# Two low parts of the up weights from VectorE to GpSimd, and the last epilogue's rows in another ring and queue: one core of Trainium2, a diffusion layer step

## The chip, the cores and the metric

The kernel runs on one core of one Trainium2 chip. The metric is the device time in microseconds (us) of one execution. Durations come from one profiled execution; the runs without a profile give the median.

## The reference

One layer of a flow-matching backbone in inference: a normalised input projection, eight heads of neighbourhood attention beside eight heads of an RWKV-7 scan, an output projection with a gated residual, and then the stage that this change touches, a gated feed-forward network with a width-3 convolution between, a residual and a last norm:

```python
D_MODEL = 1024
SEQ = 256
DEC_SEQ = 2048
D_FF = 2816
...
def _rmsnorm(x, g):
    xf = x.astype(jnp.float32)
    y = xf * lax.rsqrt(jnp.mean(xf * xf, axis=-1, keepdims=True) + EPS)
    return (y * g.astype(jnp.float32)).astype(x.dtype)
...
def _conv_ffn(h, w1, w3, wc, w2):
    return (jax.nn.silu(_dwconv(h @ w1, wc)) * (h @ w3)) @ w2
...
    h2 = _rmsnorm(x, norm2) * (1 + sc2) + sh2
    x = x + g2 * _conv_ffn(h2, *fp)
...
    y_prompt = _rmsnorm(xp, norm_f)
    y_sample = _rmsnorm(xs, norm_f)
```

`_dwconv` is the convolution of width 3 along the tokens; context (256) and latent tokens (2048) go through the same weights. All inputs and outputs are fp32. The kernel keeps fp32 accuracy on TensorE by splitting each operand of a product into a high part in the shorter format fp32r and a low part, the rest: three matmuls, high x high, low x high and high x low, stand for one.

## The kernel before, in words

Stages run one after the other; the feed-forward stage, `ffn`, takes the last 1760 us. It goes over three blocks of 768 tokens (`b`), and in each over 22 groups of 128 hidden features (`f`).

For one f, `up` (L447) makes both projections at once with seven products of quarter matrices in place of eight (a Strassen scheme), each of 4 x 3 matmuls: 84 matmuls at L456, out of sums of quarters of the weights (`PRODUCTS` names them: 11, S2, S1, 12, S3, S4, 22). VectorE puts the results together at L465 to L474, GpSimd one at L475. Of these L465 frees the PSUM tile into which a later product goes. Then `gate` (L477): the convolution `conv3` (ACT at L114, VectorE at L116), Silu on ACT (L481), the gate product on VectorE (L483, L484), and the split of the result into `gh` (ACT, L36) and `gl` (VectorE, L46). `down` (L492) multiplies it with the rows of w2: six token tiles of 6 matmuls (L499), whose PSUM tiles VectorE adds to `yacc` (L507; at a block's first f it copies them, L505). The down of f is issued behind the up of f + 1.

`UpWeights.fetch` (L334) loads the weights of the next f on the sync queue, into a ring of three tiles `wr`: r1 (columns of w1, L339), r3 (columns of w3, L340), r2 (rows of w2, L342). r1 is the quarters 11 and 12, r3 is 21 and 22. GpSimd makes the sums S1 to S4 (L354, L355, L357, L361), partly in place. `put` splits each of the seven weights: ACT writes the high part `wh` (L36), and the engine that `put` is given subtracts it to get the low part `wl` (L46). GpSimd also makes the low part `w2l` of the w2 rows. `wh` and `wl` have eight tiles each.

`tokens` (L386) prepares the next block's activations (`hT`, `lT`, `h`, `l`) when a block begins, out of `part` tiles: a ring `st` of six tiles of 128 x 512, which `up` uses as well.

`epilogue` (L421) ends a block: for each of six token tiles and two halves it loads the rows of x with `short` (L427) on the GpSimd queue into one of two tiles `e` (and, for the first two token tiles, the gate's rows), multiplies yacc by the gate (L437), adds x (L438), squares and sums on ACT (L439, which writes into the x tile, so that tile is free only then), and scales by the norm (L440 to L443). L444 stores it on the sync queue. For blocks 0 and 1 these steps are generated between the down tiles of f = 1 of the next block; for block 2 they come behind everything.

The order of instructions on each engine is not the written one: a list scheduler of the tile framework decides it, so that an edit of one engine's work can move that of others. Each engine runs its own row in order, and waits where an operand or a free tile isn't there.

Of the kernel before, what the change touches and what calls it, by code (L numbers as in the profile page):

```python
# [7 lines left out]
F32 = mybir.dt.float32  # L8
# [34 lines left out]
def split(hi_eng, lo_eng, hi, lo, src):  # L43

    copy(hi_eng, hi, src)
    lo_eng.tensor_sub(lo, src, hi)  # L46
# [15 lines left out]
class Weights:  # L62
# [21 lines left out]
    def fetch(self):  # L84

        self.load()
        if not self.raw:
            return
        r = self.raw.pop(0)
        hi = self.pool.tile([128, KT, 128], F32R, name="wh", bufs=self.ahead + 1)  # L90
        lo = self.pool.tile([128, KT, 128], F32R, name="wl", bufs=self.ahead + 1)
        split(self.nc.scalar, self.lo_eng, hi, lo, r)
        self.ready.append((hi, lo))
# [52 lines left out]
def xrows(xp, xs, t):  # L146

    return xp[t * 128 : t * 128 + 128, :] if t < 2 else xs[(t - 2) * 128 : (t - 1) * 128, :]
# [177 lines left out]
class UpWeights:  # L326
# [7 lines left out]
    def fetch(self, f):  # L334

        nc, pool, KH = self.nc, self.pool, KT // 2
        cols = slice(f * 128, f * 128 + 128)
        r1, r3, r2 = (pool.tile([128, KT, 128], F32, name="wr", bufs=3) for _ in range(3))
        nc.sync.dma_start(r1, self.wv[0][:, :, cols])  # L339
        nc.sync.dma_start(r3, self.wv[1][:, :, cols])  # L340
        r2 = r2.rearrange("p c f -> p (c f)")
        nc.sync.dma_start(r2, self.w2[cols, :])  # L342
        a11, a12, a21, a22 = r1[:, :KH], r1[:, KH:], r3[:, :KH], r3[:, KH:]
        out = {}

        def put(n, src, eng):
            h = pool.tile([128, KH, 128], F32R, name="wh", bufs=AHEAD)
            l = pool.tile([128, KH, 128], F32R, name="wl", bufs=AHEAD)
            split(nc.scalar, eng, h, l, src)
            out[n] = (h, l)  # L350

        s3 = pool.tile([128, KH, 128], F32, name="s3", bufs=1)
        put("11", a11, nc.vector)
        nc.gpsimd.tensor_sub(s3, a11, a21)  # L354
        nc.gpsimd.tensor_add(a21, a21, a22)  # L355
        put("S1", a21, nc.gpsimd)
        nc.gpsimd.tensor_sub(a21, a21, a11)  # L357
        put("S2", a21, nc.gpsimd)
        put("12", a12, nc.vector)
        put("S3", s3, nc.gpsimd)  # L360
        nc.gpsimd.tensor_sub(a12, a12, a21)  # L361
        put("S4", a12, nc.gpsimd)
        put("22", a22, nc.gpsimd)
        w2h = pool.tile([128, D], F32R, name="w2h")
        w2l = pool.tile([128, D], F32R, name="w2l")
        split(nc.scalar, nc.gpsimd, w2h, w2l, r2)
        self.ready.append((out, (w2h, w2l)))


def ffn(tc, W, rows_d, eps, wc, norm_f, h2, x1_d, yp, ys):  # L370
    nc = tc.nc
    hv = h2.rearrange("(k c p) n -> k p c n", k=2, p=128)
    KH = KT // 2
    with tc.tile_pool(name="c1", bufs=1) as c1, tc.tile_pool(name="c2", bufs=2) as c2, tc.tile_pool(
        name="cp", bufs=1, space=PSUM
# [6 lines left out]
        def part(n):  # L382

            return c2.tile([128, 512], F32, name="st", bufs=6)[:, :n]
# [36 lines left out]
        def epilogue(b, yacc):  # L421

            halves = [slice(q * 512, q * 512 + 512) for q in range(2)]

            def short(src):
                t = c2.tile([128, 512], F32, name="e")
                nc.gpsimd.dma_start(t, src)  # L427
                return t

            for t in range(6):  # L430
                tok = b * 6 + t
                y = yacc[t]
                r = c2.tile([128, 4], F32, name="rf")
                for q, s in enumerate(halves):
                    g = g2[:, s] if tok >= 2 else short(rows_d[3, 0:1, s].to_broadcast([128, 512]))
                    x = short(x1_d[tok * 128 : tok * 128 + 128, s])
                    nc.vector.tensor_mul(y[:, s], y[:, s], g)  # L437
                    nc.vector.tensor_add(y[:, s], y[:, s], x)  # L438
                    nc.scalar.activation(x, y[:, s], AF.Square, accum_out=r[:, q : q + 1])  # L439
                nc.vector.tensor_add(r[:, 2:3], r[:, 0:1], r[:, 1:2])  # L440
                nc.scalar.activation(r[:, 3:4], r[:, 2:3], AF.Sqrt, bias=eps, scale=1.0 / D)
                nc.vector.reciprocal(r[:, 2:3], r[:, 3:4])
                nc.vector.scalar_tensor_tensor(y, y, r[:, 2:3], nf, op0=ALU.mult, op1=ALU.mult)  # L443
                nc.sync.dma_start(xrows(yp, ys, tok), y)  # L444
                yield
# [1128 lines left out]
```

## Time and profile before

| what | us |
|---|---|
| median of three runs | 4527.84 (4527.21 to 4528.01) |
| profiled execution | 4528.56 |
| its span on the core | 4526.8 |
| TensorE busy in the span | 3852.0 |
| feed-forward stage | about 2767 to 4527 |
| one f in block 0, in blocks 1 and 2 | 25.42, 23.35 |

Engines: PE is TensorE's matmul, PEld its weight load, DVE is VectorE, POOL is GpSimd, SP (SPq) the sync engine's queue. A line such as L456 is that of the kernel before. The time of one f is the distance of two equal instructions of neighbouring f's. Busy shares are averages over stages with different limits, so the stretches are shown apart below.

### The profile page before, as it was taken

How to read it: one execution, taken by the hardware profiler on the slowest of the kernel's cores; microseconds unless marked ns; L12 is line 12 of the kernel's file. 1: busy time of each engine (PE TensorE's matmuls, PEld its weight loads, DVE VectorE, ACT ScalarE, POOL GpSimd, SP SyncE). 2: the span in 40 equal slices, each digit the busy share in tenths (PEclk: the TensorE clock that was granted, in tenths of full speed). 3: DMA queues.
4: the chain of work that ended last, by engine and by line, in shares of the span. 5: the costliest groups of instructions: out<-in, count | busy, mean ns of one | idle time of the engine just before them, and what ended most of it. 6: DMA issues, size and time to landing. Idle time of an engine off the chain costs nothing. (4 is left out here: it accounts for less than half of the span.)

```text
span 4526.8 us, 78134 instructions
## 1 busy us (share of the span) xinstructions
PE 3852.0 (85%) x29954; PEld 3414.9 (75%) x29954; DVE 3115.0 (69%) x4658; ACT 1845.9 (41%) x3728; POOL 2323.6 (51%) x1879
## 2 busy tenths in 40 slices
PE   6798987888388887899886886999988999889996
PEld 6787877777266666788775665888877999779995
DVE  4325586868577774566664224888888888878887
ACT  2421254544377773455442223333334333343332
POOL 0334344545234336555664444666656776667662
PEclk9899998989599997999998997999988999999998
DMA  5787545453756623323343443221223222232222
GB/s 211 243 280 212 145 117 165 114 159 112 178 116 135 128 58 102 86 76 81 95 102 105 167 149 94 61 66 61 66 80 112 68 64 70 84 106 63 70 70 66
DMA packets 682387, 513.24 MB, mean 113 GB/s; under 512 B 234691, under 2 KB 612612, under 8 KB 677916
## 3 DMA queue, kind: packets, MB, share of 16 engines
q1 hardware_dynamic: 508444, 378.64, 30.0%
q10 hardware_dynamic: 170080, 118.06, 8.8%
q0 software_dynamic: 3488, 11.54, 0.8%
q8 instruction: 236, 3.87, 0.4%
q14 instruction: 139, 1.14, 0.1%
HBM read 369.85 MB, written 139.76 MB: 113 GB/s over the span
## 5 line engine op out<-in xcount | busy, mean ns | idle before, releaser
L46 POOL TENSOR_TENSOR wl<-wr,wh 128x512 fp32r<-128x512 f32 (+1 forms) x349 | 613.2, 1758 | 575.3 <-ACT wh L36 503.8
L55 PE MATMUL g<-h,wh 128*128 128x384 f32 (+1 forms) x2592 | 641.8, 359 | 32.3 <-DVE r L116 8.4
L36 ACT ACTIVATE wh<-wr 128x512 fp32r<-128x512 f32 (+1 forms) x485 | 336.3, 704 | 500.2 <-DMA wr<-in_w_ffn_dram 210.1
L55 PEld LDWEIGHTS g<-h,wh 128*128 128x128 f32 x2592 | 487.6, 200 | 67.1 <-issue 27.7
L507 DVE TENSOR_TENSOR yacc<-yacc,yp 128x512 f32<-128x512 f32 x756 | 479.3, 680 | 28.9 <-PE yp L499 5.2
L456 PE MATMUL u<-hT,wh 128*128 128x386 f32 x1056 | 366.8, 347 | 38.3 <-DVE st L465 24.8
L456 PE MATMUL u<-lT,wh 128*128 128x386 f32 x1056 | 364.4, 345 | 12.2 <-DVE lT L46 12.2
L456 PE MATMUL u<-hT,wl 128*128 128x386 f32 x1056 | 364.4, 345 | 3.8 <-POOL wl L46 3.8
L55 PE MATMUL g<-h,wl 128*128 128x384 f32 (+1 forms) x1296 | 359.9, 355 | 0.0
L499 PE MATMUL yp<-w2h,gh 128*128 128x512 f32 x792 | 273.1, 418 | 48.6 <-DVE yacc L507 20.0
L46 DVE TENSOR_TENSOR wl<-wr,wh 128x512 fp32r<-128x512 f32 (+1 forms) x136 | 251.9, 1853 | 63.2 <-ACT wh L36 63.1
L456 PE MATMUL u<-h,wh 128*128 128x386 f32 x792 | 272.7, 344 | 19.3 <-ACT h L36 17.5
L456 PE MATMUL u<-l,wh 128*128 128x386 f32 x792 | 271.7, 345 | 8.2 <-DVE l L46 7.9
L456 PE MATMUL u<-h,wl 128*128 128x386 f32 x792 | 274.4, 346 | 0.0
L499 PE MATMUL yp<-w2l,gh 128*128 128x512 f32 x792 | 257.8, 404 | 0.0
L499 PE MATMUL yp<-w2h,gl 128*128 128x512 f32 x792 | 257.0, 403 | 0.0
L55 PEld LDWEIGHTS g<-h,wl 128*128 128x128 f32 x1296 | 250.8, 200 | 2.8 <-issue 2.5
L456 PEld LDWEIGHTS u<-hT,wh 128*128 128x128 f32 x1056 | 203.0, 192 | 51.8 <-DVE st L465 31.9
L499 PEld LDWEIGHTS yp<-w2h,gh 128*128 128x128 f32 x792 | 151.6, 193 | 108.9 <-DVE yacc L507 50.1
L354 POOL TENSOR_TENSOR s<-wr 128x512 f32<-128x512 f32 x66 | 85.8, 1300 | 271.3 <-DMA wr<-in_w_ffn_dram 271.3
L456 PEld LDWEIGHTS u<-lT,wh 128*128 128x128 f32 x1056 | 203.4, 193 | 17.8 <-DVE lT L46 17.5
L1273 DVE TENSOR_TENSOR X<-iv,mmask 128x256 f16<-128x256 f32 x360 | 146.3, 422 | 98.7 <-PE iv L1270 93.8
(333 smaller groups left out, 10085.3 us busy)
## 6 DMA issues: line engine op xcount, KB each, us to landing
wr<-in_w_ffn_dram SPq DMA_DIRECT2D x198, 512.0 KB
wr<-in_w_in_dram ACTq DMA_DIRECT2D x45, 512.0 KB
wr<-in_w_in_dram ACTq DMA_DIRECT2D x72, 256.0 KB
d_ar<-ar SPq DMA_DIRECT2D x24, 768.0 KB
d_bk<-bk SPq DMA_DIRECT2D x24, 768.0 KB
kd<-d_ks SPq DMA_DIRECT2D x32, 576.0 KB
bk<-d_bk SPq DMA_DIRECT2D x72, 256.0 KB
ar<-d_ar SPq DMA_DIRECT2D x288, 64.0 KB
```

What stands on the lines that cost most here:

```text
L36: eng.activation(dst, src, AF.Copy, scale=1.0 if scale is None else scale)
L46: lo_eng.tensor_sub(lo, src, hi)
L55: nc.tensor.matmul(ps[q][:, : e - a], A[:, c, :], B[c][:, a:e], start=c == 0 and n == 0, stop=c == KT - 1 and n == 2)
L354: nc.gpsimd.tensor_sub(s3, a11, a21)
L456: nc.tensor.matmul(acc[q], A[a][x][:, c, :], T[t][c][y], start=i < 3 and c == 0 and n == 0, stop=c == KH - 1 and n == 2, skip_group_check= ...
L499: nc.tensor.matmul(yps[q], A[:, t * 128 : t * 128 + 128], B[:, q * 512 : q * 512 + 512], start=n == 0, stop=n == 2)
L507: nc.vector.tensor_add(d, d, yps[q])
L1273: nc.vector.tensor_mul(half(X1, n), X, mk)
```

## The change

In `fetch` the low parts of the weights "11" and "12" are made by GpSimd, as those of the five others are. In `epilogue` the rows of x of the last block (b = 2) are loaded by the sync queue into the ring of six `st` tiles; in blocks 0 and 1 they stay in two `e` tiles on the GpSimd queue. The lines from L426 on are one higher in the changed kernel.

```diff
--- before.py
+++ after.py
@@ -350,13 +350,13 @@
             out[n] = (h, l)
 
         s3 = pool.tile([128, KH, 128], F32, name="s3", bufs=1)
-        put("11", a11, nc.vector)
+        put("11", a11, nc.gpsimd)
         nc.gpsimd.tensor_sub(s3, a11, a21)
         nc.gpsimd.tensor_add(a21, a21, a22)
         put("S1", a21, nc.gpsimd)
         nc.gpsimd.tensor_sub(a21, a21, a11)
         put("S2", a21, nc.gpsimd)
-        put("12", a12, nc.vector)
+        put("12", a12, nc.gpsimd)
         put("S3", s3, nc.gpsimd)
         nc.gpsimd.tensor_sub(a12, a12, a21)
         put("S4", a12, nc.gpsimd)
@@ -423,8 +423,9 @@
             halves = [slice(q * 512, q * 512 + 512) for q in range(2)]
 
             def short(src):
-                t = c2.tile([128, 512], F32, name="e")
-                nc.gpsimd.dma_start(t, src)
+
+                t = part(512) if b == 2 else c2.tile([128, 512], F32, name="e")
+                (nc.sync if b == 2 else nc.gpsimd).dma_start(t, src)
                 return t
 
             for t in range(6):
```

On VectorE, one f in the middle of block 0, around the gate product. `u_34468` is the PSUM tile that L465 empties, `t_34408` the gate's tile of this f, `t_34626` that of the next. Before:

```order
L507 TENSOR_TENSOR yacc_31746<-yacc_31746,yp_34398 128x512
L507 TENSOR_TENSOR yacc_31746<-yacc_31746,yp_34399 128x512
L46 TENSOR_TENSOR wl<-wr,wh 128x512
L483 TENSOR_TENSOR t_34408<-st,t_34408 128x386
L484 TENSOR_TENSOR t_34408<-st,t_34408 128x382
L46 TENSOR_TENSOR gl<-t_34408,gh 128x768
L465 TENSOR_TENSOR st<-st,u_34468 128x386
L46 TENSOR_TENSOR wl<-wr,wh 128x512
L116 SCALAR_TENSOR_TENSOR t_34626<-u_34467,wct,t_34626 128x255
L470 TENSOR_TENSOR st<-st,u_34468 128x386
```

and in the changed kernel (L484, L485, L466 and L471 are L483, L484, L465 and L470 of before):

```order
L508 TENSOR_TENSOR yacc_31746<-yacc_31746,yp_34398 128x512
L508 TENSOR_TENSOR yacc_31746<-yacc_31746,yp_34399 128x512
L484 TENSOR_TENSOR t_34408<-st,t_34408 128x386
L485 TENSOR_TENSOR t_34408<-st,t_34408 128x382
L46 TENSOR_TENSOR gl<-t_34408,gh 128x768
L466 TENSOR_TENSOR st<-st,u_34468 128x386
L116 SCALAR_TENSOR_TENSOR t_34626<-u_34467,wct,t_34626 128x255
L471 TENSOR_TENSOR st<-st,u_34468 128x386
```

Both `wl` are gone from the row, so that the first L483 stands right behind the additions to yacc; the rest keeps its order.

On GpSimd, the round of one f near the end of block 0 (`s_36610` is the tile of S3, L475 the addition that `up` gives to GpSimd). Before:

```order
L354 TENSOR_TENSOR s_36610<-wr 128x512
L355 TENSOR_TENSOR wr<-wr 128x512
L46 TENSOR_TENSOR w2l<-wr,w2h 128x1024
L46 TENSOR_TENSOR wl<-wr,wh 128x512
L357 TENSOR_TENSOR wr<-wr 128x512
L46 TENSOR_TENSOR wl<-wr,wh 128x512
L361 TENSOR_TENSOR wr<-wr 128x512
L46 TENSOR_TENSOR wl<-s_36610,wh 128x512
L46 TENSOR_TENSOR wl<-wr,wh 128x512
L475 TENSOR_TENSOR st<-st 128x386
L46 TENSOR_TENSOR wl<-wr,wh 128x512
```

and in the changed kernel:

```order
L354 TENSOR_TENSOR s_36610<-wr 128x512
L355 TENSOR_TENSOR wr<-wr 128x512
L46 TENSOR_TENSOR w2l<-wr,w2h 128x1024
L46 TENSOR_TENSOR wl<-wr,wh 128x512
L357 TENSOR_TENSOR wr<-wr 128x512
L46 TENSOR_TENSOR wl<-wr,wh 128x512 x2
L361 TENSOR_TENSOR wr<-wr 128x512
L46 TENSOR_TENSOR wl<-s_36610,wh 128x512
L46 TENSOR_TENSOR wl<-wr,wh 128x512
L476 TENSOR_TENSOR st<-st 128x386
L46 TENSOR_TENSOR wl<-wr,wh 128x512 x2
```

The low part of "12" stands beside that of S2 (x2), ahead of L361, and that of the next f's "11" beside that of "22" at the end, where the round waits for the load that L354 reads.

On GpSimd, in the transition from block 0 to block 1, where the epilogue of block 0 loads its rows (L427). Before:

```order
L354 TENSOR_TENSOR s_37310<-wr 128x512
L355 TENSOR_TENSOR wr<-wr 128x512
L46 TENSOR_TENSOR w2l<-wr,w2h 128x1024
L427 DMA e<-d_rows 128x512
L427 DMA e<-d_x_64 128x512
L427 DMA e<-d_rows 128x512
L475 TENSOR_TENSOR st<-st 128x386
L427 DMA e<-d_x_64 128x512 x8
L46 TENSOR_TENSOR wl<-wr,wh 128x512
L357 TENSOR_TENSOR wr<-wr 128x512
L46 TENSOR_TENSOR wl<-wr,wh 128x512
L427 DMA e<-d_x_64 128x512
```

and in the changed kernel (L428 is L427 of before):

```order
L354 TENSOR_TENSOR s_37310<-wr 128x512
L355 TENSOR_TENSOR wr<-wr 128x512
L46 TENSOR_TENSOR wl<-wr,wh 128x512
L357 TENSOR_TENSOR wr<-wr 128x512
L46 TENSOR_TENSOR w2l<-wr,w2h 128x1024
L46 TENSOR_TENSOR wl<-wr,wh 128x512
L428 DMA e<-d_rows 128x512
L46 TENSOR_TENSOR wl<-wr,wh 128x512
L361 TENSOR_TENSOR wr<-wr 128x512
L428 DMA e<-d_x_64 128x512
L46 TENSOR_TENSOR wl<-s_37310,wh 128x512
L428 DMA e<-d_rows 128x512
```

Before, eight loads of x stand in a row ahead of the weights of f = 2; now the low parts and sums of that f are mixed with the loads. On the sync queue the end changes too: behind the last weights come ten loads of x, the first store of yacc, two loads and the other five stores, where before there were six stores.

## Rows read from the trace of the kernel before

**Rows 1.** The page's first table: busy time, share of the span and instructions of each engine.

```profile
PE 3852.0 (85%) x29954; PEld 3414.9 (75%) x29954; DVE 3115.0 (69%) x4658; ACT 1845.9 (41%) x3728; POOL 2323.6 (51%) x1879
```

**Rows 2.** The busy time of each engine in six stretches of the span: block 0 from f = 2 on, the change from block 0 to 1, block 1, the change from block 1 to 2, block 2, and the end behind the last matmul. Columns: stretch, its us, then busy us (and instructions) of PE, PEld, DVE, ACT and POOL, the mean granted clock of TensorE, the DMA engines' busy share and GB/s.

```profile
2830.00:3337.00 507.00, 480.85 (x2398) 429.79 (x2397) 418.51 (x540) 171.47 (x282) 315.76 (x221) 1.00 0.21 64
3337.00:3461.00 124.00, 90.43 (x362) 75.35 (x362) 105.34 (x151) 52.37 (x101) 67.01 (x59) 0.79 0.37 119
3461.00:3905.00 444.00, 443.94 (x2280) 409.86 (x2279) 376.14 (x475) 160.85 (x268) 312.63 (x210) 1.00 0.23 69
3905.00:4069.00 164.00, 127.14 (x568) 110.71 (x567) 133.76 (x188) 69.17 (x130) 98.53 (x77) 0.89 0.30 96
4069.00:4428.00 359.00, 359.00 (x1837) 330.40 (x1836) 306.29 (x389) 126.14 (x212) 249.29 (x169) 1.00 0.23 70
4493.00:4527.00 34.00, 0.00 (x0) 0.00 (x0) 22.03 (x40) 10.99 (x29) 4.83 (x9) 0.54 0.51 170
```

**Rows 3.** The chain of waits that ended last: two rows of block 0, then two of block 1. Columns: start in us, us, what.

```profile
3237.28 2.72 DVE wl L46
3262.70 2.72 DVE wl L46
3718.51 14.90 PE u L456 x84
3733.41 8.45 PE yp L499 x36
```

**Rows 4.** What TensorE waited for in 2970 to 3330 us (block 0, 14 f's). Columns: engine, tile and line that waited, what it waited for: us in total, times, longest us. PEld is the weight load that stands ahead of a matmul.

```profile
PE u L456 <- DVE st L465: 16.9, 14, 1.2
PEld yp L499 <- DVE yacc L507: 11.8, 28, 0.5
```

**Rows 5.** The timeline of ACT and VectorE in one f of block 0. Columns: start in us, us, engine, line, operation, out<-in, shapes, count, and in brackets the idle time before it and what ended it.

```profile
3236.87 0.83 ACT L481 ACTIVATE t<-t 128x768 f32<-128x768 f32 x1
3237.20 2.80 DVE L46 TENSOR_TENSOR wl<-wr,wh 128x512 fp32r<-128x512 f32 x1
3239.92 1.64 DVE L483 TENSOR_TENSOR t<-st,t 128x386 f32<-128x386 f32 x1
```

**Rows 6.** The timeline of one f of block 1 on GpSimd, on the sync queue (SPq), ACT and VectorE; columns as in the group before.

```profile
3740.22 1.29 POOL L354 TENSOR_TENSOR s<-wr 128x512 f32<-128x512 f32 x1 [4.08 <-DMA wr<-in_w_ffn_dram]
3750.97 1.54 POOL L46 TENSOR_TENSOR wl<-wr,wh 128x512 fp32r<-128x512 f32 x1 [1.95 <-ACT wh L36]
3753.14 1.30 POOL L361 TENSOR_TENSOR wr<-wr 128x512 f32<-128x512 f32 x1 [0.63 <-DVE wl L46]
3763.66 1.30 POOL L354 TENSOR_TENSOR s<-wr 128x512 f32<-128x512 f32 x1 [4.15 <-DMA wr<-in_w_ffn_dram]
3756.97 0.37 SPq L339 DMA_DIRECT2D wr<-in_w_ffn_dram  x1
3759.54 0.37 SPq L340 DMA_DIRECT2D wr<-in_w_ffn_dram  x1
3743.57 0.85 ACT L481 ACTIVATE t<-t 128x768 f32<-128x768 f32 x1 [0.61 <-DVE t L116]
3761.12 0.63 ACT L36 ACTIVATE wh<-wr 128x512 fp32r<-128x512 f32 x1 [4.99 <-PE yp L499]
3746.22 1.64 DVE L483 TENSOR_TENSOR t<-st,t 128x385 f32<-128x385 f32 x1
```

**Rows 7.** The low parts of the up weights in 2830 to 4428 us. The first two rows are groups by line and shape: busy us, mean ns of one, idle time before and what ended it; the other two are of the view of one tile: count, duration in ns min/median/max, first and last start.

```profile
L46 POOL TENSOR_TENSOR wl<-wr,wh 128x512 fp32r<-128x512 f32 x248 | 361.4, 1458 | 111.0 <-ACT wh L36 111.0
L46 DVE TENSOR_TENSOR wl<-wr,wh 128x512 fp32r<-128x512 f32 x124 | 236.9, 1910 | 28.5 <-ACT wh L36 28.5
L46 POOL TENSOR_TENSOR wl<-wr,wh x248: 1267/1302/2278, 2833.2 to 4420.8; 128x512 fp32r<-128x512 f32 x124
L46 DVE TENSOR_TENSOR wl<-wr,wh x124: 666/1260/2899, 2831.1 to 4414.4; 128x512 fp32r<-128x512 f32 x124
```

**Rows 8.** The timeline in the two transitions: three waits of TensorE and two low parts on VectorE; columns as in Rows 5.

```profile
3452.91 1.39 PE L499 MATMUL yp<-w2h,gh 128*128 128x512 f32 x2 [7.16 <-DVE yacc L507]
3449.23 1.27 DVE L46 TENSOR_TENSOR wl<-wr,wh 128x512 fp32r<-128x512 f32 x1 [4.50 <-ACT wh L36]
3997.38 0.69 PE L456 MATMUL u<-hT,wl 128*128 128x386 f32 x1 [3.14 <-POOL wl L46]
4021.53 0.80 PE L499 MATMUL yp<-w2h,gh 128*128 128x512 f32 x1 [6.32 <-DVE yacc L507]
4017.54 1.27 DVE L46 TENSOR_TENSOR wl<-wr,wh 128x512 fp32r<-128x512 f32 x1 [5.24 <-ACT wh L36]
```

**Rows 9.** Waits in the first transition (two rows, 3337 to 3461 us) and in the second (one row, 3905 to 4069); columns as in Rows 4.

```profile
PE yp L499 <- DVE yacc L505: 11.5, 4, 5.7
POOL e L427 <- ACT e L439: 18.8, 9, 3.9
PE yp L499 <- DVE yacc L505: 8.0, 4, 5.6
```

**Rows 10.** Waits in the last epilogue, 4490 to 4527 us; columns as in Rows 4.

```profile
POOL e L427 <- ACT e L439: 46.6, 10, 28.0
DVE yacc L438 <- DMA e<-d_x: 4.8, 6, 1.5
DVE rf L440 <- ACT e L439: 2.5, 3, 0.8
```

## Prediction

> **What bounds the kernel now.** The page's first table comes first: TensorE is busy 85% of the span, VectorE 69%, GpSimd 51% [rows 1]. That is an average, and the change touches only the feed-forward stage, the last 1760 us, so the next view is the busy time by stretch [rows 2]. The reader is to see three kinds of stretch there. In block 1, 2280 matmuls fill 443.94 of 444 us, 0.1947 us for each, and in block 2 TensorE is busy for all of 359: nothing but fewer or shorter matmuls helps these. In block 0, 2398 matmuls at 0.1947 us would need 466.9 us and have 507, so 40.1 us are lost. In the two transitions 362 x 0.1947 = 70.5 stands against 124 us and 568 x 0.1947 = 110.6 against 164: 53.5 and 53.4 us lost. Behind 4493 TensorE has nothing left and VectorE is busy for 22.03 of 34 us.
>
> The chain of waits says what holds each [rows 3]. In block 1 it runs through 14.90 us of up matmuls and 8.45 us of down matmuls, which is one f in 23.35 us. In block 0 it comes round a low part on VectorE, from 3237.28 to 3262.70: 25.42 us for one f. The waits of TensorE over 14 of those f's give the difference [rows 4]: 16.9/14 = 1.21 us before the up matmuls that need L465, 11.8/14 = 0.84 us before the down tiles that need L507. Together that is 2.05, against 25.42 - 23.35 = 2.07.
>
> **Part 1: the low parts in block 0.** VectorE loses two low parts in each f. The one that counts is that of "11": it starts at 3237.20 and takes 2.80 us, L483 follows at 3239.92, and L465, for which TensorE waits, is queued behind L483, L484 and the low part of the gate. Silu, the other thing that L483 needs, has ended at 3236.87 + 0.83 = 3237.70 [rows 5]. Without the low part all of that row moves up by 3239.92 - 3237.70 = 2.2 us, more than the 1.21 us that TensorE waits: this wait goes whole. The next in line is the other wait, 0.84 us. L507 stands there behind the convolution's L116, whose order the change leaves alone, and those start from TensorE's own last product, so I take it to stay. The stretch holds 507/25.42 = 20 f's: 20 x 1.21 = 24 us. The ends: 0, if the second wait grows by what the first loses; 20 x 2.07 = 41 us, if both go and TensorE alone sets 23.35 us.
>
> **Part 2: the low parts in blocks 1 and 2, priced at nothing.** TensorE waits for nothing there, so VectorE's relief wins nothing, and the question is what GpSimd's extra work costs. Its cover is the idle time of GpSimd's loop, which is closed by loads: r3 is issued at 3759.54 when the low part of "22" is done, lands 4 us later, and L354 starts the next round, at 3740.22 and again at 3763.66 [rows 6]: 23.44 us, paced by TensorE. Two waits lie inside. The 0.63 us before L361 is a wait for VectorE's low part of "12", which now stands in GpSimd's own row: -0.63 + 1.30. The 1.95 us before the low part of S2 is ACT's: the high part stands behind the gate's high part, that behind L484, L484 behind L483. Silu ends at 3744.42, L483 starts at 3746.22, held by the low part of "11"; with that gone, all comes 1.8 us earlier. The low part of "11" falls into the gap while r3 loads: r1 is issued at 3756.97, its high part ends at 3761.12 + 0.63 = 3761.75, and 1.30 us more is 3763.05, before 3763.66. The loop then needs 23.44 - 0.63 + 1.30 - 1.8 = 22.3 us, 1.0 under TensorE's 23.35: hidden. If that cover goes, see the rivals.
>
> How long a moved part takes beside others is the weakest number here. Alone the row gives 0.67 us on VectorE and 1.27 on GpSimd (the shortest ones), while in the stage as it is the means are 1.91 and 1.46 [rows 7]: the parts on VectorE are the ones that suffer. By the shortest ones VectorE loses 124 x 0.67 = 83 us of work and by the means 237; GpSimd gains 124 x 1.27 = 157 to 124 x 1.46 = 181. I take 1.30, the median of GpSimd's own, since the moved parts fall beside the same work. The Trainium skill, GPSIMD Engine Reference, section 4.1, speaks against this move: elementwise work on two inputs belongs on VectorE, as GpSimd is about twice as slow. The shortest ones agree with it (1.9 times), the means are reversed; by the rule alone the move would add more than it takes away, by the means it takes away more.
>
> **Part 3: the transitions**, in which the epilogue of the block before runs between the down tiles of f = 1. Three of TensorE's waits end on a low part that the change takes out of the way [rows 8]: 7.16 us at 3452.91 and 6.32 at 4021.53, where L507 stood behind a low part on VectorE that itself sat waiting 4.50 and 5.24 us for ACT, and 3.14 us at 3997.38, for a low part that stood behind the loads of epilogue rows in GpSimd's row. In the new order no low part is in VectorE's row and those of the next weights stand among the loads: 16.6 us. TensorE also runs half of these stretches at the lower of its levels, 1.2 in place of 2.4 GHz (mean granted clock 0.79 and 0.89 [rows 2]), behind its waits; busy time is 90.43 - 70.5 + 127.14 - 110.6 = 36.5 us longer than at the upper level, and 16.6 is 24% of the other 70.4 us of the two losses (53.5 + 53.4 - 36.5), so 24% of 36.5 = 8.6 us more. Against that, the epilogue's loads now wait behind low parts, one or two of 1.3 us in each transition: -3. Sum: 22 us. The ends are far apart, as the old trace can't show the new order. Above: all waits for L505 go too, 11.5 + 8.0 us [rows 9], 42 us in all. Below: the loads wait for all four new low parts of the two f's in a transition, 5.2 us, and the ACT waits behind them stretch by as much again: -20 us. I take 22, nearest to the three rows that name the low part.
>
> **Part 4: the last epilogue.** The loads wait for a free tile of two, and VectorE waits 4.8 us in all for the rows of x [rows 10]. With twelve loads in a ring of six on the sync queue, which has issued its last weights long before, the first six stand ready when the down matmuls end, and the others follow as ACT frees tiles. The stores stand behind the loads in that queue, but the last store behind none that is late. 5 us; at least 0 (the sync queue's order holds a load back), at most 4.8 + 2.5 = 7.3, if VectorE's waits for ACT go too. The start of the stage is reordered by a few instructions: nothing, GpSimd waits there for loads.
>
> **Sum.** 24 + 0 + 22 + 5 = 51 us from 4528.56 gives 4477.6. The three runs' median lies 0.7 us under the profiled execution, so **4477 us**.
>
> **Rivals.**
> 1. The transitions give nothing: the loads behind low parts cost what the freed waits give. For it: GpSimd's waits in the first transition are already those for ACT to release the tiles, 18.8 us [rows 9]. 51 - 22 = 29: 4499.
> 2. Both full ends: block 0 falls to 23.35 us and the transitions give 42. 41 + 42 + 5 = 88: 4440. For it: the new order has up matmuls between the down tiles.
> 3. One of the two covers of part 2 is gone. If S2's wait stays: 23.44 - 0.63 + 1.46 = 24.27 us; if "11" does not fit the gap: 22.3 + 1.46 = 23.8. Some 35 f's (444/23.35 = 19 in block 1, 359/23.35 = 15 and one behind them in block 2) lose 0.92 or 0.45 us, 32 or 16, and block 0 gains 20 x 1.15 = 23 or 24. With part 3 and 4: 4510 or 4493.
> 4. Slower: GpSimd's loop becomes the bound because both covers are gone. 23.44 - 0.63 + 2 x 1.46 = 25.73 us: 35 x 2.38 = 83 and 20 x 0.31 = 6 us lost, 27 won: 4590. It decides from 35(p - 23.35) + 20(p - 25.42) = 27, a loop of p = 24.6 us. For it: GpSimd's work for one f grows by 2.6 us, and its means swell beside VectorE. Against it: 4 us of the loop are a load, under which one of the parts fits. The rule of the Trainium skill named above is on this rival's side.
> 5. No visible change: block 0's second wait takes the place of the first, and the transitions give nothing: 4523. Against it: the L116 row follows TensorE.
>
> **Chances.** Forecast 0.48 (its own range 4458 to 4490), rival 1 0.17, rival 2 0.14, rival 3 0.09, rival 4 0.07, rival 5 0.05. The range leaves out rivals 4 and 5 and a little at either side: 4440 to 4510. About 0.2%, 9 us, is what a measurement of this kernel can tell from no change. Faster by more: all of the forecast and rivals 1 to 3 except a little, 0.86; within: 0.06; slower: 0.08.
>
> **What would show it.** Right: a period of about 24.2 us in block 0 with no wait of TensorE for L465, still 23.35 in blocks 1 and 2; no wait of 6 to 7 us for L507 in the transitions, and these 10 us shorter each; GpSimd idle for about 1 us more than the load before some instruction of the loop; no wait for rows of x behind the last matmul. Wrong: a TensorE wait for a low part of GpSimd's in blocks 1 and 2 (rivals 3 and 4), a period over 25 us in block 0 (rival 5), or transitions that have new waits for L505 of the old size (rival 1).

## The result, and the profile after

The changed kernel takes **4473.98 us** (median of four runs, 4472.6 to 4480.61), beside 4527.52 for the kernel before (again four runs); the ratio is 0.9887, with a 95% interval of 0.9872 to 0.9902. The forecast was 4477 us, in 4440 to 4510. The profiled execution's span fell from 4526.8 to 4473.3 us, by 53.5. Its page begins with this row, which answers to [rows 1]:

```profile
PE 3829.8 (86%) x29954; PEld 3409.3 (76%) x29954; DVE 2922.4 (65%) x4526; ACT 1863.3 (42%) x3728; POOL 2476.8 (55%) x1999
```

VectorE has lost 193 us of work and GpSimd has gained 153. The same six stretches as in [rows 2], at the places where they now lie:

```profile
2830.00:3298.00 468.00, 468.00 (x2411) 433.40 (x2410) 345.62 (x504) 176.23 (x282) 366.98 (x262) 1.00 0.23 69
3298.00:3420.00 122.00, 88.60 (x388) 77.10 (x387) 109.16 (x140) 54.22 (x106) 86.13 (x72) 0.89 0.37 120
3420.00:3860.00 440.00, 438.67 (x2239) 402.31 (x2238) 310.68 (x437) 164.61 (x263) 344.93 (x242) 1.00 0.23 68
3860.00:4020.00 160.00, 127.23 (x558) 110.38 (x557) 134.90 (x179) 69.05 (x128) 111.22 (x82) 0.88 0.32 101
4020.00:4384.00 364.00, 364.00 (x1860) 334.13 (x1859) 255.93 (x361) 133.16 (x214) 287.67 (x204) 1.00 0.23 69
4448.00:4473.30 25.30, 0.00 (x0) 0.00 (x0) 21.19 (x40) 10.23 (x29) 0.00 (x0) 0.53 0.50 187
```

Block 0 now looks like block 1: TensorE busy all the time. The low parts, now all on GpSimd, take 1.41 us on average, less than 1.46 before [rows 7], although there are half as many again:

```profile
L46 POOL TENSOR_TENSOR wl<-wr,wh 128x512 fp32r<-128x512 f32 x372 | 522.0, 1410 | 190.3 <-ACT wh L36 190.0
```

Each f is marked by its L465, so the trace can be cut at equal f's. What each stretch gained is the difference of the two traces, beside the term of the prediction:

| stretch, from L465 of f to f (counted over all blocks) | before, us | after, us | gained | forecast |
|---|---|---|---|---|
| to f = 2 | 2838.8 | 2840.1 | -1.3 | 0 |
| block 0, 2 to 21 | 482.4 | 442.7 | 39.7 | 24 |
| transitions, 21 to 27 and 43 to 49 | 194.3 + 195.3 | 188.4 + 192.4 | 8.8 | 22 |
| blocks 1 and 2, 27 to 43 and 49 to 65 | 746.0 | 749.6 | -3.6 | 0 |
| 65 to the end | 70.1 | 60.2 | 9.9 | 5 |
| sum | 4526.8 | 4473.3 | 53.5 | 51 |

The sum is right within 2.5 us, and no term is: block 0 gave 15.7 more, the transitions 13.2 less, the end 4.9 more, and blocks 1 and 2, priced at nothing, lost 3.6. That the first two nearly cancel is luck. The experiments ask why.

The chain of waits (start in us, us, what), two rows of block 0 and two of block 1, answers to [rows 3]:

```profile
3220.26 8.41 PE yp L500 x36
3228.67 14.90 PE u L457 x84
3574.24 8.55 PE yp L500 x36
3582.79 14.90 PE u L457 x84
```

One f is 8.41 + 14.90 = 23.31 us in block 0: there the first wait of [rows 4] and the second, which was to stay, are both gone. In block 1 the down matmuls take 8.55 in place of 8.45, and this f 23.45 us.

### The profile page after: what moved, and what is told of

Its sections match the earlier page's. It is cut to its first block, busy times and chain, and to the rows that moved or that the text cites. A ratio compares the mean times of both kernels' runs of the same rounds, so it can differ in the third digit from the quotient of the medians.

```text
span 4473.3 us, 78133 instructions
## 1 busy us (share of the span) xinstructions
PE 3829.8 (86%) x29954; PEld 3409.3 (76%) x29954; DVE 2922.4 (65%) x4526; ACT 1863.3 (42%) x3728; POOL 2476.8 (55%) x1999
## 5 line engine op out<-in xcount | busy, mean ns | idle before, releaser
L46 POOL TENSOR_TENSOR wl<-wr,wh 128x512 fp32r<-128x512 f32 (+1 forms) x481 | 781.8, 1631 | 671.5 <-ACT wh L36 608.2
L500 PE MATMUL yp<-w2h,gh 128*128 128x512 f32 x792 | 265.5, 408 | 29.4 <-DVE yacc L506 19.2
L46 POOL TENSOR_TENSOR w2l<-wr,w2h 128x1024 fp32r<-128x1024 f32 x66 | 170.1, 2577 | 83.0 <-ACT w2h L36 83.0
L1027 POOL TENSOR_TENSOR o<-u 64x128 f32<-64x128 f32 x144 | 64.6, 453 | 267.1 <-DVE u L1023 267.1
L500 PEld LDWEIGHTS yp<-w2h,gh 128*128 128x128 f32 x792 | 150.2, 191 | 78.3 <-DVE yacc L506 22.3
```

What stands on the lines that cost most here:

```text
L500: nc.tensor.matmul(yps[q], A[:, t * 128 : t * 128 + 128], B[:, q * 512 : q * 512 + 512], start=n == 0, stop=n == 2)
L1027: nc.gpsimd.tensor_add(out, sides[0], sides[1])
```

## The experiments

In all of them a "period" is the distance of L465 from f to f, and a transition is cut as in the table above. Lines in the diffs are those of the kernel before.

**1 and 2. Each half of the change alone.** Only the two low parts moved:

```diff
-        put("11", a11, nc.vector)
+        put("11", a11, nc.gpsimd)
-        put("12", a12, nc.vector)
+        put("12", a12, nc.gpsimd)
```

> Both low parts moved to GpSimd, the last epilogue as before (two e tiles, GpSimd queue). If the two halves of the change simply add and the end is worth the 9.9 us read between the last f's of the two traces: 4474 + 10 = 4484 us, block 0 at 23.3 us for one f, blocks 1 and 2 at 23.45. If the end is worth only the 5 us of the prediction: 4479.

Only the last epilogue:

```diff
-                t = c2.tile([128, 512], F32, name="e")
-                nc.gpsimd.dma_start(t, src)
+                t = part(512) if b == 2 else c2.tile([128, 512], F32, name="e")
+                (nc.sync if b == 2 else nc.gpsimd).dma_start(t, src)
```

> Low parts as before, only the last epilogue's rows in the ring of six by the sync queue. Additive theory: 4527.5 - 10 = 4518 us, all periods as before (25.4 and 23.35). Prediction's own term: 4522. Rival, that the end only gains because the last f's run earlier beside it: no change, 4527.

Measured: 4486.81 us (ratio 0.9911, 0.9896 to 0.9925) and 4520.08 (0.9985, 0.9975 to 0.9994). By stretches the halves add: from f = 65 to the end it is 70.7 us in run 1, with the old epilogue, and 61.6 in run 2, with the new one, beside 70.1 before; block 0 is 442.7 us and 482.3. The end is worth 8.5 us by the trace of run 2 and 6.3 by its median, so the rival "no change" is out. The medians gain 39.6 and 6.3 us, 45.9 together beside 53.5 for the change; the profiled execution of run 1 reaches f = 2 at 2844.3 us, 4.2 later than that of the change and ahead of all that was edited, so not all of that gap belongs to the edits.

**3 and 4. Each low part alone**, with the new last epilogue:

```diff
-        put("11", a11, nc.vector)
+        put("11", a11, nc.gpsimd)
```

> The changed kernel with only the low part of 11 moved; that of 12 stays on VectorE. Theory of the prediction: the part of 11 (2.8 us ahead of the gate product) is what held block 0, so its period falls to 24.2 or lower, and the time is 4475 to 4493 us. Rival: VectorE's load as a whole counts; then the period falls by half, to about 24.35, and this kernel and the one with only 12 moved are alike, about 4495 both.

```diff
-        put("12", a12, nc.vector)
+        put("12", a12, nc.gpsimd)
```

> The changed kernel with only the low part of 12 moved; that of 11 stays on VectorE. Theory: block 0 keeps 25.4 us, as the part of 11 still stands ahead of the gate product; 4518 us plus or minus what the transitions do. Rival (VectorE's load as a whole): about 24.35 us in block 0 and 4495.

Measured: **4528.31 us** (ratio 1.0005, 0.9995 to 1.0014) and **4539.36** (1.0029, 1.0017 to 1.0042). Neither theory had this. Run 2, with the same epilogue and neither part moved, took 4520.08, so each half of the move takes more than it gives. With 11 alone block 0 falls from 25.39 to 23.82 us for one f, as the prediction's step says, but blocks 1 and 2 rise to 24.0 and 23.9, and the transitions from 194.3 and 195.3 to 197.9 and 206.2. With 12 alone the period is 24.85 in block 0, where 25.4 was expected, and 24.1 and 24.0 in blocks 1 and 2.

With 11 alone, the chain of waits of one f in block 1 (start, us, what) is this:

```profile
3645.97 2.08 DVE t L116 x2
3648.05 0.47 DVE st L474
3648.52 0.53 DVE t L116
3649.04 1.20 DVE yacc L507 x2
3650.29 5.63 PE yp L499 x23
```

TensorE's down matmuls wait for L507, L507 for the instructions ahead of it in VectorE's row, and the first two of those, L116, take 2.08 us. GpSimd's and VectorE's timelines at this place (start, us, engine, line, operation, shapes) say why:

```profile
3645.36 1.03 POOL L475 TENSOR_TENSOR st<-st 128x386 f32<-128x386 f32 x1
3646.34 1.29 POOL L46 TENSOR_TENSOR wl<-wr,wh 128x512 fp32r<-128x512 f32 x1
3645.97 0.62 DVE L116 SCALAR_TENSOR_TENSOR t<-u,wct,t 128x386 f32<-128x386 f32 x1 [0.69 <-ACT t L114]
3646.51 1.54 DVE L116 SCALAR_TENSOR_TENSOR t<-st,wct,t 128x382 f32<-128x382 f32 x1
```

The second L116 reads st and t, both from SBUF. It is next when GpSimd's low part of 22 has just begun, at 3646.34. That one ends at 3647.63, and L116 at 3646.51 + 1.54 = 3648.05, 0.42 later. The first L116, which reads u from PSUM, takes 0.62 beside the same GpSimd row. In the changed kernel the same three instructions are:

```profile
3573.49 1.01 POOL L476 TENSOR_TENSOR st<-st 128x386 f32<-128x386 f32 x1
3574.47 1.61 POOL L46 TENSOR_TENSOR wl<-wr,wh 128x512 fp32r<-128x512 f32 x1
3573.93 0.99 DVE L116 SCALAR_TENSOR_TENSOR t<-st,wct,t 128x382 f32<-128x382 f32 x1
```

Here L116 comes while GpSimd's addition L476 still runs, to 3574.50; it ends at 3574.92, again 0.42 later, and now the low part of 22 is the one that takes longer, 1.61 us. So the two engines hardly ran such instructions side by side: the later one had most of its work still to do when the earlier one ended. With no GpSimd instruction beside it the same L116 takes 0.61 us (run 5), so 0.42 us behind GpSimd's end means that about 0.2 of it were done by then. The Trainium skill, GPSIMD Engine Reference, section 1 (Specifications), says that GpSimd shares its SBUF interfaces with VectorE, with contention where VectorE has two SBUF inputs; these rows agree, and show the price, up to most of the other's instruction.

The same holds for the 2.80 us low part of 11 in [rows 5], the main term of the prediction. One f later in the kernel before, it stands beside the low part of the w2 rows:

```profile
3262.46 2.41 POOL L46 TENSOR_TENSOR w2l<-wr,w2h 128x1024 fp32r<-128x1024 f32 x1 [2.26 <-ACT w2h L36]
3262.61 2.80 DVE L46 TENSOR_TENSOR wl<-wr,wh 128x512 fp32r<-128x512 f32 x1
```

`w2l` ends at 3264.87 and the low part of 11 at 3265.41, 0.54 later; so it is, to 0.03 us, in all 19 f's from f = 2 to 21. The shortest of its kind took 0.67 [rows 7]. The low part that held block 0 was itself held by GpSimd.

With 12 alone it is GpSimd's row that holds TensorE (timelines of GpSimd, ACT and VectorE, one f of block 1):

```profile
3655.18 2.81 POOL L46 TENSOR_TENSOR wl<-wr,wh 128x512 fp32r<-128x512 f32 x2 [1.95 <-ACT wh L36]
3658.06 1.29 POOL L361 TENSOR_TENSOR wr<-wr 128x512 f32<-128x512 f32 x1
3659.39 1.16 ACT L36 ACTIVATE wh<-wr 128x512 fp32r<-128x512 f32 x2 [2.40 <-POOL wr L361]
3661.08 0.62 DVE L116 SCALAR_TENSOR_TENSOR t<-u,wct,t 128x386 f32<-128x386 f32 x1 [1.64 <-ACT t L114]
```

GpSimd waits 1.95 us for the high part of S2, held by VectorE's low part of 11 as in [rows 6]; ACT waits for L361, its convolution step L114 stands behind those high parts, and L116 behind that. The L116 that took 1.54 us in run 3 takes 0.67 here, so this is another cause. It is the first case of rival 3, "S2's wait stays", worked out at 24.27 us and measured at 24.1 and 24.0.

**5. Without the low part of 22**, in the kernel with 11 alone:

```diff
-        put("22", a22, nc.gpsimd)
+        h22 = pool.tile([128, KH, 128], F32R, name="wh", bufs=AHEAD)
+        nc.scalar.activation(h22, a22, AF.Copy)
+        out["22"] = (h22, out["S4"][1])
```

> The kernel with only the low part of 11 moved, and without the low part of 22: that product reads the low part of S4 in its place, so GpSimd makes one low part less in each f and that part of the result is wrong by the size of a low part. Theory (the convolution's L116 from SBUF waits while GpSimd's low part of 22 runs, and L507 and TensorE behind it): the L116 of 382 columns falls from 1.54 to about 0.65 us, and the period of blocks 1 and 2 from 24.00 to 23.35 us, that of block 0 from 23.81 to 23.3. Rival (TensorE is paced by VectorE's low part of 12 or by something on ACT): still 24.0.

Measured: 23.29 us in block 0, 23.32 and 23.25 in blocks 1 and 2 (one run, 4483.75 us; the transitions stay long, 195.6 and 198.2). The L116 in question, by line and shape (busy us, mean ns): first the kernel before, block 0 and block 1, then the changed one, then that with 11 alone, then this one in block 1:

```profile
L116 DVE SCALAR_TENSOR_TENSOR t<-st,wct,t 128x381 f32<-128x381 f32 x13 | 20.9, 1610 | 0.0
L116 DVE SCALAR_TENSOR_TENSOR t<-st,wct,t 128x382 f32<-128x382 f32 x12 | 8.0, 666 | 0.0
```

```profile
L116 DVE SCALAR_TENSOR_TENSOR t<-st,wct,t 128x381 f32<-128x381 f32 x13 | 12.7, 978 | 0.0
L116 DVE SCALAR_TENSOR_TENSOR t<-st,wct,t 128x382 f32<-128x382 f32 x12 | 12.1, 1004 | 0.0
```

```profile
L116 DVE SCALAR_TENSOR_TENSOR t<-st,wct,t 128x381 f32<-128x381 f32 x14 | 21.1, 1509 | 0.0
L116 DVE SCALAR_TENSOR_TENSOR t<-st,wct,t 128x382 f32<-128x382 f32 x12 | 18.6, 1550 | 0.0
```

```profile
L116 DVE SCALAR_TENSOR_TENSOR t<-st,wct,t 128x382 f32<-128x382 f32 x12 | 7.3, 607 | 0.0
```

So where the L116 takes 1.5 to 1.6 us TensorE waits behind it; at 1.0 us TensorE waits 0.1 in blocks 1 and 2 and hardly in block 0; at 0.6 not at all. Run 5 also takes work from GpSimd, but GpSimd's load is not the cause: in the kernel with 11 alone it waits 2.9 us for TensorE's down matmuls, by way of ACT, ahead of `w2l`, and in run 9 below it has less to do than in the change and the period is longer.

**6. L475 on VectorE**, in the kernel with 11 alone, so that the low part of 22 runs earlier and VectorE has more to do:

```diff
-            nc.gpsimd.tensor_add(u3, u3, m5)
+            nc.vector.tensor_add(u3, u3, m5)
```

> The kernel with only the low part of 11 moved, and with the addition L475 given to VectorE in place of GpSimd: GpSimd's low part of 22 then runs 1 us earlier, ahead of the long L116, with more work on VectorE and the same low parts. Theory (who runs beside L116): L116 of 382 columns about 0.7 us, period 23.4 in blocks 1 and 2, 4500 us. Rival (VectorE's load counts): period over 24, 4530 or more.

Measured: periods of 23.27 and 23.4 us, so the theory holds with GpSimd's low parts unchanged and more work on VectorE; L116 takes 0.90 us, not 0.7:

```profile
L116 DVE SCALAR_TENSOR_TENSOR t<-st,wct,t 128x382 f32<-128x382 f32 x12 | 10.8, 897 | 0.0
```

The time, 4488.97 us (ratio 0.9911, 0.9896 to 0.9926), is 11 under the number expected, with transitions of 202.7 and 191.4.

**7. One more low part for GpSimd**, in the changed kernel:

```diff
         put("S4", a12, nc.gpsimd)
+        nc.gpsimd.tensor_sub(out["S4"][1], a12, out["S4"][0])
```

> The changed kernel with the low part of S4 computed twice: one more low part of 1.3 us for GpSimd in each f. If its loop has the slack that the idle times in the trace after give (1.26 us before w2l and 0.74 before S2, so up to 2 us): period unchanged at 23.3 and 23.45, 4474 us within 10. If the loop already is the bound of blocks 1 and 2 (23.45 against 23.35): period 24.7 there, 4474 + 35 x 1.3 = 4520.

Measured: 4582.04 us (ratio 1.0117, 1.01 to 1.0134), period 25.0 in all blocks. The first theory has too much slack, the second the wrong reason, since 23.45 was not the loop. In the changed kernel GpSimd still waits 1.15 us ahead of w2l for TensorE's pace, so its loop needs 23.45 - 1.15 = 22.3 us, the sum that part 2 of the prediction had:

```profile
3583.97 2.71 POOL L46 TENSOR_TENSOR w2l<-wr,w2h 128x1024 fp32r<-128x1024 f32 x1 [1.15 <-ACT w2h L36]
```

One part more makes it 25.0, so it cost 2.7 and not 1.3 us. The chain (three of its rows) shows part of the rest: r1, whose last reader is the added instruction, and r3 are now asked for one behind the other, and r3 needs 4.88 us instead of about 4:

```profile
3705.34 1.26 POOL wl L46
3706.61 4.88 DMA wr<-in_w_ffn_dram
3711.56 1.29 POOL s L354
```

The rest was not told apart. The margin of the changed kernel is under one instruction, and one instruction further the chip shows something near rival 4's 25.73 us and 4590.

**8. The middle epilogues' rows on the sync queue as well:**

```diff
-                (nc.sync if b == 2 else nc.gpsimd).dma_start(t, src)
+                nc.sync.dma_start(t, src)
```

> The changed kernel with the epilogue rows of blocks 0 and 1 on the sync queue as well (still two tiles). Theory (the transitions lose because GpSimd's weights and the epilogue's loads stand in one row): the waits of TensorE in the transitions shrink by the 10 us of GpSimd's waits for a free row tile, 4464. Rival (the next weights' loads now stand behind the row loads on the sync queue): transitions longer by as much, 4484.

Measured: 4472.56 us (4469.75 to 4479.12), between the two and not to be told from the change; but the transitions are 184.2 and 189.8 us, 6.7 less in all, while f = 2 came 3.8 later in this execution. Whether these 6.7 us are the shared row's is not shown. Run 1, whose middle epilogue is the change's own, has 3.7 less as well; and of the two other pairs of kernels that differ in this queue alone, one gives 7.2 (run 10 beside 9) and one nothing (run 11 beside 6, 0.6 more).

**9, 10 and 11. In search of a better one.** L475 on VectorE in the changed kernel (9); that with all rows on the sync queue (10); 11 alone, L475 on VectorE, all rows on the sync queue (11). Their edits are those above.

> The changed kernel with the addition L475 on VectorE. Theory: GpSimd's low part of 22 is past when the long L116 comes, so blocks 1 and 2 fall from 23.45 to 23.35 us for one f, 35 x 0.1 = 3.5 us, and block 0 stays at 23.3: 4470 us, if the transitions keep their length. Rival (the 0.1 us are GpSimd's loop itself, or a longer matmul): 23.45 as before.

> The changed kernel with L475 on VectorE and the epilogue rows of blocks 0 and 1 on the sync queue. If the two add: 3.5 us from the periods and the 6.7 us by which the transitions were shorter with the sync queue, 4464 us. If each new order of the scheduler shifts the transitions by as much as such an edit is worth: anywhere between 4460 and 4490, with the periods at 23.3 and 23.35 all the same.

> Only the low part of 11 on GpSimd, L475 on VectorE, and all epilogue rows on the sync queue. The kernel with the first two had periods of 23.27 and 23.37 us and transitions of 202.7 and 191.4; the two kernels with the rows on the sync queue had transitions of 184 to 190. If the transitions follow the queue: 442 + 187 + 374 + 187 + 372 + 61 us behind the 2843 at which f = 2 starts, a span of 4466 us, 4468 us in all, 6 below the change. If they follow the scheduler's order of the moment: 4470 to 4490, with the same periods.

Measured: 4512.83, 4502.83 and 4490.2 us (ratios 0.9965, 0.9947 and 0.9916, each with an interval of 0.0014 to either side). In 9 and 10 the periods rose to 23.89 in block 0 and 24.05 in block 1, against every expectation: the earlier low part came, but just at the wrong moment (rows of run 9):

```profile
3673.99 2.54 POOL L46 TENSOR_TENSOR wl<-wr,wh 128x512 fp32r<-128x512 f32 x2
3675.35 1.60 DVE L116 SCALAR_TENSOR_TENSOR t<-st,wct,t 128x382 f32<-128x382 f32 x1
```

The pair of low parts is S4's and 22's; the second begins at 3675.24, 0.11 us ahead of L116, which then takes 1.60. The same L116 in block 0 takes 1.58 us in run 9 and 1.51 in run 3, and the periods, 23.89 and 23.82, differ by the same 0.07. In 11 the periods are 23.27 and 23.34, but its transitions are 198.7 and 196.0 us, as the rival theory had it. No kernel here beats the change by more than can be told.

## Why the prediction came out right

**Part 1, block 0: right, and too small.** The low part of 11 did hold block 0, and the first wait went. The step that failed is "the convolution's L116, whose order the change leaves alone": their order stayed, but not their length, which fell from 1.61 to 0.98 us. Before, GpSimd's low part of 22 fell on the 381-column L116 of block 0; in the changed kernel GpSimd's round lies later against TensorE's, and it no longer does. Here are the two in the kernel before, then in the changed one:

```profile
3251.57 1.31 POOL L46 TENSOR_TENSOR wl<-wr,wh 128x512 fp32r<-128x512 f32 x1
3251.66 1.63 DVE L116 SCALAR_TENSOR_TENSOR t<-st,wct,t 128x381 f32<-128x381 f32 x1
```

```profile
3219.68 0.96 DVE L116 SCALAR_TENSOR_TENSOR t<-st,wct,t 128x381 f32<-128x381 f32 x1
3220.19 1.61 POOL L46 TENSOR_TENSOR wl<-wr,wh 128x512 fp32r<-128x512 f32 x1
```

GpSimd came 0.09 us ahead of L116 before and comes 0.51 behind it now; a shift of 0.6 us decided over this wait, and that it went the right way was luck, as nothing in the prediction foresaw it. With both waits gone block 0 gave 39.7 us in 19 f's, 2.09 for each: the whole of the upper end (2.07). Runs 3 and 5 show this: with the long L116 (11 alone) 23.82 us, without it 23.29.

**Part 2, blocks 1 and 2: the loop right, the price not nothing.** GpSimd's loop is 22.3 us, as worked out. But by the same contention the L116 of block 1 grew from 0.67 to 1.00 us, and 0.1 us for each f made 3.6 us. Run 4 shows that the cover of S2's wait does hang on the low part of 11 leaving VectorE, as worked out. Run 3 loses as much in these blocks without GpSimd's loop being the bound, by the L116 of 1.55 us, which the prediction does not have.

**Part 3, the transitions: mis-sized, 8.8 us for 22.** The three waits that were named are gone, and GpSimd's waits for a free row tile fell from 18.8 [rows 9] to 5.0 us in the first transition. The clock's term, 8.6 us, came to 4.8: TensorE's busy time above 0.1947 us for each matmul fell from 36.5 to 31.6, and the mean granted clock from [rows 2] to now went from 0.79 to 0.89 and from 0.89 to 0.88. (The lower level held some 42% and 22% of the stretches by the old means, not the half that the prediction names.) What is left of the waits, two rows of the first transition, then one of the second (us in total, times, longest):

```profile
POOL e L428 <- ACT e L440: 5.0, 2, 3.8
PE yp L500 <- DVE yacc L506: 7.6, 4, 3.0
PE yp L500 <- DVE yacc L506: 11.6, 3, 6.4
```

TensorE's waits for L505 (now L506) fell in the first from 11.5 [rows 9] to 7.6 and grew in the second from 8.0 to 11.6: 19.2 us in place of 19.5, the prediction's own sign for rival 1. And a new wait came in the first. Rows of ACT, VectorE and TensorE there:

```profile
3352.37 0.63 ACT L36 ACTIVATE wh<-wr 128x512 fp32r<-128x512 f32 x1 [1.83 <-POOL wr L357]
3352.90 0.83 ACT L482 ACTIVATE t<-t 128x768 f32<-128x768 f32 x1
3353.76 1.31 DVE L484 TENSOR_TENSOR t<-st,t 128x385 f32<-128x385 f32 x1 [4.30 <-ACT t L482]
3364.74 0.69 PE L457 MATMUL u<-hT,wh 128*128 128x386 f32 x1 [8.17 <-DVE st L471]
```

ACT's row holds Silu behind a high part that waits 1.83 us for GpSimd's L357; VectorE then sits 4.30 us, its epilogue steps bunch up ahead of L471, and TensorE waits 8.17 us. So a low part no longer stands in the way in VectorE's row, but GpSimd's sums do by way of ACT's. The prediction also left out what the low parts do to VectorE from GpSimd's side. The epilogue's L437 and L438 have two SBUF inputs, as the L116 above has. First transition, before and then now (busy us, mean ns):

```profile
L438 DVE TENSOR_TENSOR yacc<-yacc,e 128x512 f32<-128x512 f32 x12 | 13.0, 1081 | 3.0 <-DMA e<-d_x 3.0
L439 DVE TENSOR_TENSOR yacc<-yacc,e 128x512 f32<-128x512 f32 x12 | 16.0, 1338 | 2.4 <-DMA e<-d_x 2.2
```

Of the 48 such steps of the two transitions, 12 took over 0.75 us before and 26 do now. VectorE lost 18.2 us of low parts in these stretches, and yet its busy time grew from 105.34 to 109.16 and from 133.76 to 134.90 us. How much of that reached TensorE no run tells, nor what the loads in GpSimd's row cost (run 8). The order that the scheduler finds for each kernel counts as well, as transitions of 184 to 206 us over the runs say. What makes up the missing 13.2 us stays open.

**Part 4, the end: 9.9 us for 5**, and 8.5 by run 2 alone. The place was right, and the bound of 7.3 too low. VectorE's waits for rows and for ACT, both in [rows 10], are gone; the only wait of VectorE that is left behind the last matmul is this:

```profile
DVE rf L443 <- ACT rf L442: 0.4, 1, 0.4
```

With all rows there, VectorE had another tile's step to do while ACT squared, so that 21.19 of the last 25.3 us are work, beside 22.03 of 34.

**The rivals.** The forecast stood because half of rival 2 came true (block 0 to its full end) and more than half of rival 1 (the transitions gave little). Rival 4 was the right danger, one instruction away (run 7). Rival 3 is what one half of the move gives (run 4). Rival 5 is out, as block 0's second wait went with the first. The rule of section 4.1 of GPSIMD Engine Reference in the Trainium skill, that elementwise work on two inputs belongs on VectorE, would have been right for run 4, where TensorE waits for GpSimd's row, and not for the whole move, which gained 39.6 us (run 1).

## What to carry to other kernels

Price a VectorE instruction with two SBUF inputs by what GpSimd runs at that moment, not by its usual length: a change that only shifts GpSimd's phase can give or take most of a GpSimd instruction in each round (0.61 to 1.63 us for the L116 here). Where two engines share a loop, test the parts of a move singly before trusting a term: here two halves that each cost time gain 40 us together. A sum can be right while every term is wrong; cut both traces at equal marks and compare term by term.

## What the runs showed of the hardware

VectorE and GpSimd hardly ran instructions side by side where VectorE's had two SBUF inputs. In blocks 0 and 1 of the change, the kernel before and runs 3 and 9, the L116 of 381 or 382 columns, with both inputs in SBUF, ended 0.40 to 0.43 us after the GpSimd instruction during which it began, whatever its own start, and took 0.66 to 1.63 us; with nothing on GpSimd beside it (run 5) it took 0.61. In run 9 a low part that began 0.11 us ahead of L116 was enough to make 1.60 us of it. VectorE instructions with one input in PSUM showed nothing of this: such an L116 took 0.62 us beside the same instructions, and L507 the same time throughout, while L438, as large but with both inputs in SBUF, took 0.67 to 3.15 us. L507 in the kernel before (ns, shortest, median and longest):

```profile
L507 DVE TENSOR_TENSOR yacc<-yacc,yp x659: 668/680/690, 2975.1 to 4427.7; 128x512 f32<-128x512 f32 x165
```
